# The first group of a streaming encoder's input projection: k by k over all three column tiles, with two weight pieces issued from ScalarE's queue

## The chip, the core and the metric

One core of a Trainium2 chip runs the whole program. The metric is the device time of one execution in microseconds (us). Five engines work side by side, each on its own row of instructions, in the order in which the program lists them: TensorE (PE, matmuls into PSUM), VectorE (DVE), ScalarE (ACT), GpSimd (POOL) and SyncE (SP), which issues nearly all DMAs of this kernel. They wait for one another through semaphores. PSUM is used as eight banks; the kernel gives six of them to the matmul results (pool `psm`) and two to small products.

## What is computed

One layer of a hybrid encoder over 2048 prompt positions and 8 x 16 sample positions, width 1024:

```python
h = jnp.einsum('btd,de->bte', x, w_in)                      # 1024 -> 2816 columns
a, g_a, u, v, g_b, c1, c2, g_c = jnp.split(h, SPLITS, axis=-1)
y_a = pool_mixer(pool_ext, a, ...)                           # trailing means, pool_w
y_b = u * spatial_mix(layer_norm(v), gmlp_w, gmlp_b)         # chunked gating
c = c1 * jax.nn.sigmoid(c2)
y_c = conformer_tail(concat(conv_left, c), conv_w, ...)      # 31 taps, LayerNorm, pointwise
mixed = concat([silu(g_a) * y_a, silu(g_b) * y_b, silu(g_c) * y_c])
x_new = layer_norm(ALPHA * x + einsum(mixed, w_out) + b_out)
```

## The kernel before

**Three products for one.** Each float32 operand is split into a high part (`xhi`, `whi`: a cast on ACT) and a low part (`xlo`, `wlo`: value minus high part, on DVE). `mm3` issues for every 128-row slice k of the contraction three matmuls per result: high times high (L208) and the two mixed ones (L209, L210). Its argument `outs` lists the results that are built together; the loop over k is outside, that over the results inside.

**Blocks and groups.** Positions go in three blocks of 768, 768 and 640; x is kept transposed in SBUF as `xhi`, `xlo` for one block. The columns of `w_in` go in eight groups (`GROUPS`); group 0 holds the column tiles c2/0, c1/0, c2/1, and group 1 holds c1/1, c2/2, c1/2. A block of 768 positions is two runs of 384 for each column tile, so one column tile of a block fills two PSUM banks.

**Evictions of c1 and c2.** `c_in` allocates the banks, issues the matmuls and then the evictions: for c2 a tanh on ACT (L474) from PSUM into `cext`; for c1 a product on DVE (L476, shown under the helper's line L131) that reads `cext` and PSUM. After c1, 31 taps of the depthwise convolution are put in a list, `fill`, from which the program hands one at a time to DVE. With one column tile in `todo`, `c_in` calls `mm3` once for each run of 384; with two, once for all their runs together.

**Weights.** A group's weights come in four pieces of two k each, through four stage buffers (tag `stage`, shared with the x rows at the start), and are split into a ring of six `whi`, `wlo` pairs. In the first block the split pieces are also stored to DRAM (`put`, L184, arrays `keep`), because the later blocks read them back. Group 0 and the x rows are loaded by code at the top (L280 to L303): `w0` is the first weight piece, loaded in two halves from inside `XRow` (its argument `mid`), between the two halves of the x rows 0 and 1. `Loader` loads the next group's pieces, and its `hook` splits the last two at given k of the last `mm3` of a group.

**What sets the order.** All engines are programmed by hand (`manual_schedule`). A planner's clock, `Clock.pe`, is moved on by `poll` after every k of `mm3`; `after(us, fn)` puts work on a list that `poll` takes from when its time has come. So what an engine's row holds, and in which order, follows from the places at which `poll` is called, and not from what is ready on the chip. The weights of the pooling mixer (`load_pool`, tile `pw`) are loaded 12 us into that plan by four DMAs on SP (L349) and split 8 us of the plan later (a cast on ACT, `poolwhi`, and a difference on DVE, `poolwlo`).

Of the kernel before, what the change touches and what calls it, by code (L numbers as in the profile page):

```python
# [11 lines left out]
AF = mybir.ActivationFunctionType  # L12
# [48 lines left out]
def splits(total):  # L61

    tiles = total // P
    n = -(-tiles // 3)
    out, t = [], 0
    for i in range(n):
        w = -(-(tiles - t) // (n - i))
        out.append((t * P, w * P))
        t += w
    return out  # L70
# [3 lines left out]
def encoder_kernel(ctx: ExitStack, tc: tile.TileContext, a):  # L74
    nc = tc.nc
# [28 lines left out]
    def drain(tag=None):  # L104

        while fill and (tag is None or any(t == tag for t, _ in fill)):
            fill.pop(0)[1]()

    def poll(us):
        Clock.pe += us  # L110
        while events and events[0][0] <= Clock.pe:
            heapq.heappop(events)[2]()
        run_fill()
# [22 lines left out]

    warm = const.tile([P, 1], F32, name="warm")
    nc.vector.memset(warm, 0.0)
    nc.scalar.activation(out=warm, in_=warm, func=AF.Silu)
    mhalf = const.tile([P, 1], F32, name="mhalf")  # L140
    nc.gpsimd.memset(mhalf, -0.5)
    onec = const.tile([P, 1], F32, name="onec")
# [20 lines left out]
    def stage():  # L163
        return core.tile([P, TMAX], F32, tag="stage", bufs=STAGE, name="stage")
# [33 lines left out]
    def wslice(key, k, c0, n):  # L198
        hi, lo = ring[key][k // 2]
        return hi[:, k % 2, c0:c0 + n], lo[:, k % 2, c0:c0 + n]  # L200

    def mm3(outs, kdim=KT, hook=None):

        for k in range(kdim):
            for ps, lhs, rhs in outs:
                lh, ll = lhs(k)
                rh, rl = rhs(k)
                nc.tensor.matmul(ps, lh, rh, start=(k == 0), stop=False)  # L208
                nc.tensor.matmul(ps, lh, rl, start=False, stop=False)  # L209
                nc.tensor.matmul(ps, ll, rh, start=False, stop=(k == kdim - 1))  # L210
            if hook is not None:
                hook(k)
            poll(sum(3 * (o[0].shape[-1] / 2400 + 0.0025) for o in outs))
        Clock.dve = max(Clock.dve, Clock.pe)
# [54 lines left out]
    def xslice(k, t0, n):  # L269
        return xhi[k // 2][:, k % 2, t0:t0 + n], xlo[k // 2][:, k % 2, t0:t0 + n]  # L270
# [10 lines left out]
    wv = a["w_in"][:, 0:KT * 384].rearrange("p (k c) -> p k c", k=KT)  # L281
    w0 = stage().rearrange("p (k c) -> p k c", k=2)
# [2 lines left out]
    ring[0, 0] = [(whi0, wlo0)]  # L285
    rows = []
    for k in range(2):
        rows.append(XRow(0, k, lambda k=k: nc.sync.dma_start(out=w0[:, k, :], in_=wv[:, k, :])))
    w1 = wg[1]()
    for k in range(2):  # L290
        nc.vector.tensor_copy(whi0[:, k, :], w0[:, k, :])
# [4 lines left out]
    for k in range(2, KT, 2):  # L296
        rows = [XRow(0, k), XRow(0, k + 1)]
# [142 lines left out]
    def prompt_width(b):  # L440
        return min(len(BLOCKS[b]), SEQ // P - BLOCKS[b][0]) * P

    def c_in(b, todo, wkey, hook=None):

        T, Tp = len(BLOCKS[b]) * P, prompt_width(b)
        runs, pss = [], {}
        for what, j, c0 in todo:
            if what == "c2":
                drain(j)
                ext = cp.tile([P, CONVC + TMAX], F32, tag=f"cext{j}", name=f"cext{j}")  # L450
                conv_state[(b, "ext", j)] = ext
                nc.gpsimd.tensor_copy(ext[:, 0:CONVC], halo_c[:, j, :])
            for t0, n in splits(T):
                ps = psm.tile([P, 512], F32, tag="mm", name="ps_c")
                pss[(what, j, t0)] = ps
                runs.append((ps[:, :n], lambda k, c0=c0: wslice(wkey, k, c0, P),
                             lambda k, t0=t0, n=n: xslice(k, t0, n)))
        if len(todo) > 1:
            mm3(runs)
        for what, j, c0 in todo:  # L460
            ext = conv_state[(b, "ext", j)]
            for t0, n in splits(T):
                if len(todo) == 1:
                    mm3([runs.pop(0)], hook=hook if t0 > 0 else None)
                ps = pss[(what, j, t0)]
                m = max(min(n, Tp - t0), 0)
                pieces = []
                if m > 0:
                    pieces.append((ext[:, CONVC + t0:CONVC + t0 + m], ps[:, :m]))
                if m < n:  # L470
                    pieces.append((exts[:, j, :, CONVC:], ps[:, m:n].rearrange("p (b t) -> p b t", b=NB)))
                for e, p in pieces:
                    if what == "c2":
                        nc.scalar.activation(out=e, in_=p, func=AF.Tanh, scale=0.5)  # L474
                    else:
                        vec.scalar_tensor_tensor(out=e, in0=e, scalar=1.0, in1=p,  # L476
                                                       op0=ALU.add, op1=ALU.mult)
            if what == "c1":
                nc.gpsimd.tensor_copy(halo_c[:, j, :], ext[:, Tp:Tp + CONVC])
                if conv_state.get("held") is None:  # L480
                    conv(b, j)
                else:
                    conv_state["held"].append(lambda j=j: conv(b, j))
# [167 lines left out]
    def spread(steps, every=STEP):  # L651

        def go():
            try:
                fn = next(steps)
            except StopIteration:
                return
            if fn is not None:
                fn()
            after(every, go)  # L660
        go()
# [179 lines left out]
    class Loader:  # L841
# [21 lines left out]
        def hook(self, plan):  # L863
            return lambda k: self.next(plan.get(k, 0))
# [3 lines left out]
    def group_work(b, g, hook):  # L868
        key, group = (b, g), GROUPS[g]
        what = group[0][0]  # L870
        if what in ("v", "gb", "u"):
            {"v": b_v, "gb": b_gate, "u": b_u}[what](b, key, hook)
        elif what in ("c1", "c2"):
            todo = [(w, j, c * P) for c, (w, j) in enumerate(group)]
            if g == 0:
                c_in(b, todo[:2], key)
                todo = todo[2:]
            for i, t in enumerate(todo):
                c_in(b, [t], key, hook if i == len(todo) - 1 else None)
        elif g == LASTG:  # L880
            c_gate(b, [(0, 0)], key)
            c_gate(b, [(1, P), (2, 2 * P)], key, hook)
        else:
            for c, (what, j) in enumerate(group):
                {"ga": a_gate, "a": a_main}[what](b, j, key, c * P, hook if c == len(group) - 1 else None)
# [3 lines left out]
    for b in range(len(BLOCKS)):  # L889
        if b > 0:  # L890
            drain()
            conv_state["held"] = []
            spread(tail_steps(b - 1))
        for g in range(LASTG):
            if b == 0 or (b, g + 1) == (LASTB, LASTG):
                loads = Loader([(fn, 1) for fn in w_in((b, g + 1), g + 1)])
                after(6, loads.next)
                after(9, loads.next)
                group_work(b, g, loads.hook({1: 1, 3: 1}))
            else:  # L900

                for i, fn in enumerate(w_kept(b, g + 1)):
                    after(10 + i if g % 2 == 0 and i < 2 else 5 + i, fn)
                group_work(b, g, None)
        if b == 0:
            W = w_kept(b + 1, 0)
            after(5, W[0])
            after(6, W[1])
            loads = Loader([(lambda k=k: XRow(b + 1, k), 1) for k in range(KT)])

            def leave(k):
                if k in (2, 4):
                    W[1 + k // 2]()
                if 2 <= k < 7:
                    loads.next()
            group_work(b, LASTG, leave)
            loads.next(3)
        elif b < LASTB:
            for i, fn in enumerate(w_kept(b + 1, 0)):
                after(5 + i, fn)  # L920
            rows = {}

            def load(*ks, b=b):
                for k in ks:
                    rows[k] = XRow(b + 1, k)

            def leave(k):
                if k in (2, 4):
                    load(k - 2, k - 1)
                if k == 5:  # L930
                    for i in range(2):
                        rows[i].split(lambda i=i: load(i + 4))
            group_work(b, LASTG, leave)
            for i in range(2, 4):
                rows[i].split(lambda i=i: load(i + 4))
            for i in range(4, KT):
                after((2.5, 3.5, 5.5, 6.5)[i - 4], lambda i=i: rows[i].split())
# [24 lines left out]
    wv = a["w_out"].rearrange("(k p) c -> p k c", p=P)  # L962
# [28 lines left out]
    loads = Loader(jobs)  # L991
# [176 lines left out]
```

## Time and profile before

| what | value |
|---|---|
| median of 3 runs | 785.02 us (785.01 to 785.61) |
| profiled execution, device time | 785.92 us |
| profiled execution, span | 784.2 us |
| PE busy, share of the span | 771.1 us, 98% |
| DVE busy, share of the span | 611.3 us, 78% |
| ACT busy, share of the span | 203.8 us, 26% |

The span runs from the first to the last instruction of the profiled execution; the device time beside it holds 1.72 us more. In a timeline row stand the start in us, the duration in us, the engine, the line, the operation with output and inputs, the count, and in brackets the idle time of the engine before it with what ended it. Matmuls overlap in time, so their pace is read from the differences of their starts. SPq is SP's queue: the time in which it issues a DMA, not that in which the data moves. PEld is the loading of the stationary operand.

### The profile page before, as it was taken

To read this page: it belongs to the slowest core of one execution; us is meant where nothing else is said; L and a number is where in the kernel's file an instruction comes from. 1 tells how busy PE (TensorE), PEld (TensorE's weight loads), DVE (VectorE), ACT (ScalarE), POOL (GpSimd) and SP (SyncE) were. 2 spreads that over 40 slices of the span, in tenths; PEclk is the share of its full clock that TensorE was granted. 3 is DMA by queue.
4 is the path that set the end of the run, shared out by engine and by line. 5 is a ranking of instruction groups with operands and counts; after the bars stand their busy time and mean duration, and the time that the engine had idled before them with its cause. 6 is when DMAs were issued, how large, how long until landed. Compare 5 with 4: busy or idle time off the path is not lost.

```text
span 784.2 us, 11348 instructions
## 1 busy us (share of the span) xinstructions
PE 771.1 (98%) x4340; PEld 732.4 (93%) x4340; DVE 611.3 (78%) x904; ACT 203.8 (26%) x380; POOL 146.3 (19%) x175
## 2 busy tenths in 40 slices
PE   8999999999999999999999999999999999999995
PEld 7999999999999999999999999999988878888885
DVE  5699999996489989896047888898764997676665
ACT  5322323222312130220142122031351243131210
POOL 1010112210011011230002200160006154232342
PEclk9999999999999999999999999999999999999999
DMA  7866856459431375413655147362477334435411
GB/s 259 329 217 189 279 218 231 160 192 344 172 109 53 81 237 187 161 55 132 230 172 199 58 103 209 134 209 97 143 230 266 108 134 162 161 116 176 137 71 61
DMA packets 74918, 132.91 MB, mean 169 GB/s; under 512 B 15600, under 2 KB 41712, under 8 KB 74864
## 3 DMA queue, kind: packets, MB, share of 16 engines
q1 hardware_dynamic: 74864, 132.19, 50.2%
q8 instruction: 34, 0.56, 0.3%
q14 instruction: 20, 0.16, 0.1%
HBM read 90.52 MB, written 41.64 MB: 169 GB/s over the span
## 4 chain that ended last, share of the span: by engine, by line
PE 87%; DVE 3%; DMA 3%; SPq 3%; ACT 1%; POOL 1%; issue 1%; POOLq 0%; DVEq 0%; ACTq 0%
PE ps_o L208 7%; PE ps_o L210 7%; PE ps_o L209 7%; PE ps_c L208 4%; PE ps_c L210 4%; PE ps_c L209 4%; PE ps_gb L208 3%; PE ps_gb L209 3%; PE ps_gb L210 3%; PE ps_v L209 3%; PE ps_v L210 3%; PE ps_v L208 3%; PE ps_u L210 3%; PE ps_u L209 3%; PE ps_u L208 3%; PE ps_gc L210 2%
## 5 line engine op out<-in xcount | busy, mean ns | idle before, releaser
L131 DVE SCALAR_TENSOR_TENSOR acc<-cext,cw,acc 128x768 f32<-128x768 f32 (+1 forms) x270 | 257.8, 955 | 4.2
L208 PE MATMUL ps_o<-woxhi,mhi 128*128 128x512 f32 (+1 forms) x208 | 81.5, 392 | 0.3 <-ACT sgc L533 0.3
L210 PE MATMUL ps_o<-woxhi,mlo 128*128 128x512 f32 (+1 forms) x208 | 80.7, 388 | 0.0
L208 PE MATMUL ps_c<-xhi,whi 128*128 128x384 f32 (+1 forms) x240 | 79.7, 332 | 0.4 <-ACT xhi L152 0.4
L209 PE MATMUL ps_o<-woxlo,mhi 128*128 128x512 f32 (+1 forms) x208 | 80.0, 385 | 0.0
L209 PE MATMUL ps_c<-xlo,whi 128*128 128x384 f32 (+1 forms) x240 | 79.1, 329 | 0.5 <-DVE xlo L131 0.5
L210 PE MATMUL ps_c<-xhi,wlo 128*128 128x384 f32 (+1 forms) x240 | 78.5, 327 | 0.0
L131 DVE TENSOR_TENSOR xlo<-stage,xhi 128x768 fp32r<-128x768 f32 (+2 forms) x26 | 21.6, 853 | 35.5 <-ACT xhi L152 35.5
L210 PEld LDWEIGHTS ps_o<-woxhi,mlo 128*128 128x128 f32 x208 | 39.0, 188 | 8.7
L209 PEld LDWEIGHTS ps_c<-xlo,whi 128*128 128x128 f32 x240 | 45.2, 188 | 1.8 <-DVE xlo L131 1.6
L208 PE MATMUL ps_u<-whi,xhi 128*128 128x384 f32 x136 | 46.6, 343 | 0.0
L208 PEld LDWEIGHTS ps_o<-woxhi,mhi 128*128 128x128 f32 x208 | 39.2, 188 | 7.9 <-ACT sgc L533 0.7
L209 PEld LDWEIGHTS ps_o<-woxlo,mhi 128*128 128x128 f32 x208 | 39.1, 188 | 8.0
L208 PEld LDWEIGHTS ps_c<-xhi,whi 128*128 128x128 f32 x240 | 45.4, 189 | 1.0 <-ACT xhi L152 0.7
L424 ACT ACTIVATE xr<-xr,onm,ors 128x1024 f32<-128x1024 f32 x16 | 19.9, 1246 | 99.9 <-POOL onm L420 99.9
L210 PE MATMUL ps_u<-whi,xlo 128*128 128x384 f32 x136 | 45.6, 335 | 0.0
L209 PE MATMUL ps_u<-wlo,xhi 128*128 128x384 f32 x136 | 45.5, 335 | 0.0
L209 PE MATMUL ps_v<-wlo,xhi 128*128 128x384 f32 x136 | 45.5, 334 | 0.0
L210 PE MATMUL ps_v<-whi,xlo 128*128 128x384 f32 x136 | 45.5, 334 | 0.0
L208 PE MATMUL ps_v<-whi,xhi 128*128 128x384 f32 x136 | 45.5, 334 | 0.0
L210 PEld LDWEIGHTS ps_c<-xhi,wlo 128*128 128x128 f32 x240 | 45.3, 189 | 0.0
L131 DVE TENSOR_TENSOR xr<-xr,ln_g 128x1024 f32<-128x1024 f32 x16 | 28.5, 1782 | 20.1 <-ACT xr L424 20.1
(216 smaller groups left out, 1947.2 us busy)
## 6 DMA issues: line engine op xcount, KB each, us to landing
whi<-keep SPq DMA_DIRECT2D x34, 384.0 KB, 5.5
wlo<-keep SPq DMA_DIRECT2D x34, 384.0 KB, 6.1
stage<-in_w_in SPq DMA_DIRECT2D x27, 384.0 KB, 5.0
keep<-whi SPq DMA_DIRECT2D x24, 384.0 KB, 3.9
keep<-wlo SPq DMA_DIRECT2D x24, 384.0 KB, 3.9
xr<-in_x_prompt SPq DMA_DIRECT2D x16, 512.0 KB, 4.8
o_y<-xr SPq DMA_DIRECT2D x16, 512.0 KB, 2.9
stage<-keep SPq DMA_DIRECT2D x20, 384.0 KB, 7.4
```

The lines of the kernel that those rows point to most:

```text
L131: return fn(*args, **kw)
L208: nc.tensor.matmul(ps, lh, rh, start=(k == 0), stop=False)
L209: nc.tensor.matmul(ps, lh, rl, start=False, stop=False)
L210: nc.tensor.matmul(ps, ll, rh, start=False, stop=(k == kdim - 1))
L424: nc.scalar.activation(out=out, in_=src, func=AF.Identity, scale=rs, bias=nm_)
```

## The change

Three edits. First, in block 0, group 0 is done by one call of `c_in` with all three column tiles: six runs, in six banks, k by k; before, the first two column tiles went k by k in four banks and the third followed by itself. `c_in` now hands its `hook` to that `mm3`. Second, the plan at which the next group's last two weight pieces are split becomes k = 5 and k = 7 of that one `mm3`; it was k = 1 and k = 3 of the last run. Third, the two halves of `w0` are issued from ACT's DMA queue and no longer from SP's, and the first activation on ACT (`warm`, a Silu of one column, which brings the loading of the activation table with it) is moved behind them.

```diff
-    nc.scalar.activation(out=warm, in_=warm, func=AF.Silu)
...
     for k in range(2):
-        rows.append(XRow(0, k, lambda k=k: nc.sync.dma_start(out=w0[:, k, :], in_=wv[:, k, :])))
+        rows.append(XRow(0, k, lambda k=k: nc.scalar.dma_start(out=w0[:, k, :], in_=wv[:, k, :])))
+    nc.scalar.activation(out=warm, in_=warm, func=AF.Silu)
...
         if len(todo) > 1:
-            mm3(runs)
+            mm3(runs, hook=hook)
...
-            if g == 0:
+            if g == 0 and b == 0:
+
+                c_in(b, todo, key, hook)
+                todo = []
+            elif g == 0:
                 c_in(b, todo[:2], key)
                 todo = todo[2:]
...
-                group_work(b, g, loads.hook({1: 1, 3: 1}))
+                group_work(b, g, loads.hook({1: 1, 3: 1} if (b, g) != (0, 0) else {5: 1, 7: 1}))
```

In the changed kernel the lines from L139 to L288 have numbers one smaller, so L207 to L209 there are the three matmuls, L151 the cast and L183 the stores of the kept weights.

On PE, at the end of the first k of group 0, the row of before reads as follows; the numbers behind `ps_c` name the banks' tiles.

```order
L208 MATMUL ps_c_235<-xhi0_110,whi_96 128x384
L209 MATMUL ps_c_235<-xlo0_111,whi_96 128x384
L210 MATMUL ps_c_235<-xhi0_110,wlo_97 128x384
L208 MATMUL ps_c_232<-xhi0_110,whi_96 128x384
L209 MATMUL ps_c_232<-xlo0_111,whi_96 128x384
L210 MATMUL ps_c_232<-xhi0_110,wlo_97 128x384
```

The same place of the changed kernel:

```order
L207 MATMUL ps_c_235<-xhi0_110,whi_95 128x384
L208 MATMUL ps_c_235<-xlo0_111,whi_95 128x384
L209 MATMUL ps_c_235<-xhi0_110,wlo_96 128x384
L207 MATMUL ps_c_238<-xhi0_110,whi_95 128x384
L208 MATMUL ps_c_238<-xlo0_111,whi_95 128x384
L209 MATMUL ps_c_238<-xhi0_110,wlo_96 128x384
L207 MATMUL ps_c_239<-xhi0_110,whi_95 128x384
L208 MATMUL ps_c_239<-xlo0_111,whi_95 128x384
L209 MATMUL ps_c_239<-xhi0_110,wlo_96 128x384
L207 MATMUL ps_c_232<-xhi0_110,whi_95 128x384
L208 MATMUL ps_c_232<-xlo0_111,whi_95 128x384
L209 MATMUL ps_c_232<-xhi0_110,wlo_96 128x384
```

Between the fourth bank and the return to the first one now stand the two banks of c2/1: a k holds 18 matmuls where it held 12, and all six banks are finished in the last k.

On ACT, around the end of group 0, the row of before with the semaphores that each instruction waits for (`cext_230` is column tile 0, `cext_364` column tile 1; `whi` of 128x768 are group 1's four pieces, `whi` of 128x2x256 the first of group 2's):

```order
L152 CAST whi<-stage 128x768 [waits DMAHW0_49]
L152 CAST whi<-stage 128x768 [waits DMAHW1_49]
L474 ACTIVATE cext_230<-ps_c 128x384 [waits PE_49] x2
L474 ACTIVATE cext_364<-ps_c 128x384 [waits PE_49]
L152 CAST whi<-stage 128x768 [waits DMAHW2_49,DMAHW4_49,DVE_49,PE_49]
L152 CAST whi<-stage 128x768 [waits DMAHW3_49,DMAHW6_49,DVE_49,PE_49]
L152 CAST poolwhi<-pw_338 128x256 [waits DMAHW6_49,DMAHW1_49,DMAHW7_49,DMAHW0_49,Pool_49]
L474 ACTIVATE cext_364<-ps_c 128x384 [waits PE_49]
L152 CAST whi<-stage 128x2x256 [waits DMAHW6_49,DMAHW2_49]
```

The same place now (`cext_236` is column tile 1):

```order
L151 CAST whi<-stage 128x768 [waits DMAHW0_49]
L151 CAST whi<-stage 128x768 [waits DMAHW1_49]
L151 CAST whi<-stage 128x768 [waits DMAHW2_49,DMAHW4_49,DVE_49,PE_49]
L151 CAST whi<-stage 128x768 [waits DMAHW3_49,DMAHW6_49,DVE_49,PE_49]
L151 CAST poolwhi<-pw_347 128x256 [waits DMAHW6_49,DMAHW1_49,DMAHW7_49,DMAHW0_49,Pool_49]
L474 ACTIVATE cext_230<-ps_c 128x384 [waits PE_49] x2
L474 ACTIVATE cext_236<-ps_c 128x384 [waits PE_49] x2
L151 CAST whi<-stage 128x2x256 [waits DMAHW6_49,DVE_49]
```

Three of the four tanh evictions have moved behind group 1's last two weight casts and behind the cast of the pool weights, which waits for the four DMAs of `pw`.

On SP, at the very start, the row of before:

```order
L257 DMA stage<-in_xT 128x384
L288 DMA stage<-in_w_in 128x384
L259 DMA stage<-in_xT 128x384
L257 DMA stage<-in_xT 128x384
L288 DMA stage<-in_w_in 128x384
L259 DMA stage<-in_xT 128x384
L172 DMA stage<-in_w_in 128x768
```

And now:

```order
L256 DMA stage<-in_xT 128x384
L258 DMA stage<-in_xT 128x384
L256 DMA stage<-in_xT 128x384
L258 DMA stage<-in_xT 128x384
L171 DMA stage<-in_w_in 128x768
```

The two weight halves are gone from SP's row. Behind this place SP's row is the same in both kernels: the rest of x and of group 0, `cst`, group 1's four pieces, ten stores of kept weights, the four DMAs of `pw`, and so on. On DVE all four differences of group 1's pieces now stand ahead of the two products of c1/0, and the first taps follow these.

## The prediction

> **What bounds the kernel now.** I read the page first: busy shares, then the chain of work that ended last.
>
> ```profile
> PE 771.1 (98%) x4340; PEld 732.4 (93%) x4340; DVE 611.3 (78%) x904; ACT 203.8 (26%) x380; POOL 146.3 (19%) x175
> PE 87%; DVE 3%; DMA 3%; SPq 3%; ACT 1%; POOL 1%; issue 1%; POOLq 0%; DVEq 0%; ACTq 0%
> ```
>
> PE is the bound: the end of the kernel moves by what PE's row of work moves, and anything else counts only through a wait of PE. So the next view is the timeline of PE over the first 62 us, where the change lies.
>
> ```profile
> 4.48 0.88 PE L208 MATMUL ps_c<-xhi,whi 128*128 128x384 f32 x1
> ...
> 6.01 0.34 PE L208 MATMUL ps_c<-xhi,whi 128*128 128x384 f32 x1
> ...
> 9.84 0.34 PE L210 MATMUL ps_c<-xhi,wlo 128*128 128x384 f32 x1
> 10.56 0.45 PE L208 MATMUL ps_c<-xhi,whi 128*128 128x384 f32 x1 [0.38 <-ACT xhi L152]
> 11.55 0.44 PE L209 MATMUL ps_c<-xlo,whi 128*128 128x384 f32 x1 [0.55 <-DVE xlo L131]
> 11.83 0.34 PE L210 MATMUL ps_c<-xhi,wlo 128*128 128x384 f32 x1
> ...
> 32.34 0.33 PE L208 MATMUL ps_c<-xhi,whi 128*128 128x384 f32 x1
> ...
> 57.30 0.33 PE L208 MATMUL ps_ga<-xhi,whi 128*128 128x384 f32 x1
> ...
> 59.56 0.34 PE L209 MATMUL ps_ga<-xlo,whi 128*128 128x384 f32 x1
> 60.33 0.44 PE L210 MATMUL ps_ga<-xhi,wlo 128*128 128x384 f32 x1 [0.43 <-DVE wlo L131]
> ```
>
> Group 1 runs from 32.34 to 57.30 without a wait: 144 matmuls in 24.96 us, 0.1733 us each. Group 0 has the same 144 and took 32.34 - 4.48 = 27.86 us, so it loses **2.90 us**. Of these, 1.01 lie in the first three matmuls (the fourth starts at 6.01, not at 5.00), 1.48 at 9.84 to 11.83 (three steps in 1.99 us where 0.52 would do), where x row 2 arrives late, and 0.4 in between. A last loss is at 60.33, 0.60 us behind its pace (0.77 after 59.56 less 0.17), on a low weight part that DVE made late. More than 3 us can't be won here.
>
> **The change, part by part.** *k by k over six banks.* A k holds 18 matmuls, 3.12 us, where it held 12, 2.08 us. Rows on DVE that end x rows 2, 4 and 7:
>
> ```profile
> 10.54 0.96 DVE L131 TENSOR_TENSOR xlo<-stage,xhi 128x768 fp32r<-128x768 f32 x1 [0.83 <-ACT xhi L152]
> ...
> 14.38 0.96 DVE L131 TENSOR_TENSOR xlo<-stage,xhi 128x768 fp32r<-128x768 f32 x1
> 20.64 0.96 DVE L131 TENSOR_TENSOR xlo<-stage,xhi 128x768 fp32r<-128x768 f32 x1 [0.78 <-ACT xhi L152]
> ```
>
> With 1.0 us lost at the start as now, k = 2 begins at 4.48 + 1.0 + 36 x 0.1733 = 11.7 and its x row is there at 11.50; k = 4 at 18.0 against 15.34, k = 7 at 27.3 against 21.60. All are met even if no row comes earlier. Group 0 then ends at 4.48 + 24.96 + 1.0 = **30.4**, a gain of 1.9.
>
> *Two issues on ACT's queue.*
>
> ```profile
> 0.78 1.28 ACT L139 ACT_TABLE_LOAD   x1 [0.78 <-PEq L1150]
> 2.08 0.20 ACT L139 ACTIVATE warm<-warm 128x1 f32<-128x1 f32 x1
> 3.21 0.51 ACT L152 CAST xhi<-stage 128x384 fp32r<-128x384 f32 x1 [0.93 <-DMA stage<-in_xT]
> ...
> 1.24 0.42 SPq L288 DMA_DIRECT2D stage<-in_w_in  x1
> ...
> 2.64 0.43 SPq L288 DMA_DIRECT2D stage<-in_w_in  x1
> ```
>
> The table load and `warm` move behind two issues of 0.42 and 0.43, to end near 3.2; ACT was idle 0.93 us there waiting for the first x half, so that cast stays near 3.2 and costs nothing, and would cost PE nothing until it slips by about 0.5. SP gives up 0.85 us, so everything behind may come 0 to 0.85 us earlier; the lower end, if the engines that move the data are full, the upper if only issuing counts. I take 0.5, since the stage buffers and the data both hold the row.
>
> *The evictions of group 0.* This is the large term. ACT's row now:
>
> ```profile
> 22.76 0.84 ACT L152 CAST whi<-stage 128x768 fp32r<-128x768 f32 x1 [0.95 <-DMA stage<-in_w_in]
> 23.50 0.87 ACT L474 ACTIVATE cext<-ps_c 128x384 f32<-128x384 f32 x2
> ...
> 30.29 0.84 ACT L152 CAST whi<-stage 128x768 fp32r<-128x768 f32 x1 [1.41 <-PE ps_c L209]
> 31.33 0.84 ACT L152 CAST whi<-stage 128x768 fp32r<-128x768 f32 x1 [0.20 <-PE ps_c L209]
> 37.12 0.41 ACT L152 CAST poolwhi<-pw 128x256 fp32r<-128x256 f32 x1 [4.95 <-DMA pw<-in_pool_w]
> 37.44 0.49 ACT L474 ACTIVATE cext<-ps_c 128x384 f32<-128x384 f32 x1
> ```
>
> ACT waits 4.95 us for the pool weights, and today that is harmless: the tanhs that free group 1's first banks ran at 23.50, ahead of it, and only one stands behind it. In the changed order the pool cast stands ahead of all four. Group 0 holds six banks of six, all unfinished until the last k, so group 1's first matmul needs the first tanh, and that needs the pool weights. When do they land?
>
> ```profile
> 22.00 1.52 SPq L184 DMA_DIRECT2D keep<-whi  x1
> ...
> 31.13 0.77 SPq L184 DMA_DIRECT2D keep<-wlo  x1
> 31.99 3.31 SPq L349 DMA_DIRECT2D pw<-in_pool_w  x4
> ...
> 24.00:32.30 8.30, 8.30 (x50) 8.30 (x49) 7.33 (x10) 2.54 (x4) 0.72 (x2) 1.00 0.99 397
> ```
>
> On SP they stand behind ten stores of kept weights (the first and the last shown), in a stretch whose DMA engines are 0.99 busy at 397 GB/s; SP's order there is unchanged, and none of those stores waits for PE. So they come when they come now, less the 0.5. The weight casts ahead of the pool cast wait for stores too, but these are ahead of `pw` on SP, and the casts had run by 32.2.
> - pool cast: 37.12 - 0.5 = 36.6; first tanh 37.44 - 0.5 = 36.94, end 37.43;
> - group 1 starts at about **37.45**: PE stands still for 37.45 - 30.4 = 7.0 us, and group 1 begins 37.45 - 32.34 = **5.1 us later** than before.
>
> Behind the waiting pool cast stand on ACT the four tanhs, then group 2's casts; on DVE the two products of c1/0, `poolwlo` and the first taps; on POOL the halo copies. Group 2's weights aren't needed until 62.
>
> *Restart of PE.* A pause of 7 us has no like in the trace. The lower bound is the pause at 9.84 to 11.83, after which the pace was full at once: 0. The upper is the start of the program:
>
> ```profile
> 3.56 0.15 PEld L277 LDWEIGHTS <-wz 128*128 128x128 bf16 x1 [0.28 <-issue]
> 3.99 0.15 PEld L277 LDWEIGHTS <-wz 128*128 128x128 bf16 x1 [0.28 <-issue]
> ...
> 1.45 3.60 PE L277 MATMUL wps<-wz 128*128 128x512 bf16 x8 [1.45 <-POOL wz L274]
> ...
> 3.75:5.00 1.25, 1.25 (x5) 0.49 (x2) 1.19 (x3) 0.02 (x1) 0.00 (x0) 1.00 0.81 230
> ```
>
> There the warm-up matmuls of 512 columns follow one another every 0.43 us, 0.32 for 384 columns where 0.173 is the later pace, and this holds from 1.45 to about 6.0: 4.55 x (1 - 0.173 / 0.32) = 2.1 us lost. Seven idle microseconds are nearer to that than to two; I take **1.9**. The granted clock speaks against it: the third number from the end of the window row is 1.00 there too, so that column doesn't show what slowed PE.
>
> The Trainium skill has a rule for it ("TensorE: Matmul & The Clock Gate", section "What's actually happening"): PE's clock falls to half after an idle window of about 3.4 us and returns after one of sustained work. By it the slow stretch would be an estimated 3.4 to 6.8 us and the loss 1.6 to 3.1; the head's pace agrees with it, the granted clock column doesn't.
>
> *The taps.* DVE starts the convolution at about 38.5 instead of 25.6. By then it had done six taps:
>
> ```profile
> 25.63 0.68 DVE L131 TENSOR_SCALAR acc<-cext,cw,cst 128x768 f32<-128x768 f32 x1
> 26.34 4.18 DVE L131 SCALAR_TENSOR_TENSOR acc<-cext,cw,acc 128x768 f32<-128x768 f32 x4
> ...
> 33.08 1.01 DVE L131 SCALAR_TENSOR_TENSOR acc<-cext,cw,acc 128x768 f32<-128x768 f32 x1
> ...
> 59.59 1.29 DVE L131 TENSOR_TENSOR wlo<-stage,whi 128x512 fp32r<-128x512 f32 x2
> ...
> 80.00:100.00 20.00, 20.00 (x118) 20.00 (x117) 19.58 (x25) 6.25 (x10) 1.99 (x3) 1.00 0.85 287
> 180.00:200.00 20.00, 20.00 (x117) 20.00 (x116) 11.08 (x13) 7.13 (x12) 0.00 (x0) 1.00 0.95 334
> ```
>
> That is 0.68 + 4.18 + 1.01 = 5.9 us put off, while PE itself is 7 us later, and in the new order seven taps fewer (17, not 24) stand ahead of the `wlo` of 59.59. So the stall of 0.60 at 60.33 should go, and the taps end in the 8.9 us that DVE idles in 180 to 200. I cost it at -0.6; without that cover it is 0.
>
> **Sum**, against the profiled execution: 785.92 + 5.1 + 1.9 - 0.6 = 792.3. That execution is 0.90 above the median of the runs, so on the median: 785.02 + 6.4 = **791.4 us**. Nothing after 62 us would win it back, PE being without slack.
>
> **The rivals.**
> - *No slow restart.* All as above, but PE resumes at full pace: 791.4 - 1.9 = **789.5**. For it: the pause at 10 us. Against it: that pause is short. Chance 0.22.
> - *DVE's backlog bites.* From 80 us DVE is nearly full, and the taps put off may stand ahead of a weight difference or of an eviction that PE waits for. The price is between the 0.6 not won back and the 5.9 put off; I take 2: **793.4**. Against it: the plan moved the taps behind those. Chance 0.12.
> - *The wait isn't there, and it is faster.* If the pool weights land early enough, PE goes on and the change brings 1.9 + 0.6: **782.5**. The point from which it decides: group 1 starting by 32.34 + 0.6, five microseconds before 37.95, that is the weights in SBUF by about 32.1. Before, SP only began to issue them at 31.99, and 0.85 is the most that the change brings forward. It needs the full DMA engines to be emptied by much more than two issues. Chance 0.07.
> - *Something between*: landing 2 to 4 us earlier, a shorter pause, no slow restart: about **786.5**. Chance 0.04.
>
> **How the numbers follow.** The forecast itself has 0.55. A measurement of this kernel tells about 0.2%, 1.6 us, from no change: faster 0.07, same 0.03, slower 0.90. The range: low end, no slow restart and the full 0.85 won, 789.5 - 0.35, less 0.35 for a start that loses 0.65 instead of 1.0: 788.8. High end: no shift (+0.5), restart 2.1 (+0.2), the stall of 60.33 kept (+0.6), and half of the first microsecond of the backlog case: 793.2. What is left out are the last two rivals and the larger part of the second.
>
> **What would show it.** Right: group 0's last matmul near 30.4 with no wait at 10 to 12; the pool cast near 36.6 with a wait for `pw` ahead of it; on PE one idle gap of about 7 us that ends on a tanh of ACT; matmuls of 384 columns every 0.32 us for some microseconds behind it; no wait on `wlo` near 66. Wrong: a pool cast before 32, a gap under 5 us, full pace at once, or PE waits for DVE after 62 us that weren't there.

## The result and the profile after

| kernel | median, us | lowest to highest | runs |
|---|---|---|---|
| before | 785.02 | 784.45 to 785.73 | 5 |
| changed | 791.75 | 790.72 to 792.17 | 5 |

The changed kernel is slower: ratio 1.0082, 95% interval 1.0070 to 1.0093. (This and the later ratios are formed over all the runs and differ a little from the quotient of two medians.) The profiled execution took 792.17 us (span 790.5), 6.25 more than the one of before (785.92, span 784.2). The page's busy shares and the shares of the chain that ended last:

```profile
PE 771.6 (98%) x4340; PEld 734.1 (93%) x4340; DVE 611.8 (77%) x904; ACT 203.2 (26%) x380; POOL 145.4 (18%) x175
PE 84%; DMA 5%; DVE 4%; POOL 2%; SPq 1%; ACT 1%; issue 1%; POOLq 0%; ACTq 0%; DVEq 0%
```

The busy times are those of before to within a microsecond (PEld: 1.7), so the 6.25 us are no added work. PE is still the bound, and DMA's share of the chain has grown from 3% to 5%. The timeline of PE says where:

```profile
4.51 0.46 PE L207 MATMUL ps_c<-xhi,whi 128*128 128x384 f32 x1
5.48 0.44 PE L208 MATMUL ps_c<-xlo,whi 128*128 128x384 f32 x1 [0.51 <-DVE xlo L131]
5.94 0.33 PE L207 MATMUL ps_c<-xhi,whi 128*128 128x384 f32 x1
...
30.23 0.34 PE L209 MATMUL ps_c<-xhi,wlo 128*128 128x384 f32 x1
37.44 0.69 PE L207 MATMUL ps_c<-xhi,whi 128*128 128x384 f32 x1 [6.87 <-ACT cext L474]
37.92 0.52 PE L208 MATMUL ps_c<-xlo,whi 128*128 128x384 f32 x1
...
41.44 0.52 PE L207 MATMUL ps_c<-xhi,whi 128*128 128x384 f32 x1
41.76 0.43 PE L208 MATMUL ps_c<-xlo,whi 128*128 128x384 f32 x1
42.03 0.34 PE L209 MATMUL ps_c<-xhi,wlo 128*128 128x384 f32 x1
42.21 0.34 PE L207 MATMUL ps_c<-xhi,whi 128*128 128x384 f32 x1
...
64.57 0.33 PE L207 MATMUL ps_ga<-xhi,whi 128*128 128x384 f32 x1
```

Group 0 ends at 30.40 (its last start, 30.23, and one step of 0.17), without the waits of 10 to 12 us. Group 1 begins at 37.44: 7.04 us of standstill, ended by a tanh of ACT. (The 6.87 in the bracket is counted from the end of the last matmul, which overlaps the next step.) Then the starts are 0.48, twelve times 0.32 and once 0.27 us apart before they are 0.17 to 0.18. Group 1 takes 64.57 - 37.44 = 27.13 us, 2.17 more than the 24.96 of before. What held the tanh stands in ACT's timeline, one row above it:

```profile
3.83 0.51 ACT L151 CAST xhi<-stage 128x384 fp32r<-128x384 f32 x1 [0.63 <-DMA stage<-in_xT]
...
29.18 0.83 ACT L151 CAST whi<-stage 128x768 fp32r<-128x768 f32 x1 [1.06 <-DMA keep<-whi]
36.59 0.41 ACT L151 CAST poolwhi<-pw 128x256 fp32r<-128x256 f32 x1 [6.57 <-DMA pw<-in_pool_w]
36.90 1.63 ACT L474 ACTIVATE cext<-ps_c 128x384 f32<-128x384 f32 x4
```

All four tanhs are queued behind the cast of the pool weights. The chain of waits between 28 and 45 us joins the pieces; a row is the start, the length and what it was:

```profile
30.07 1.04 SPq L349
...
32.05 0.59 SPq L349
32.64 0.04 issue
32.68 3.76 DMA pw<-in_pool_w
...
36.59 0.41 ACT poolwhi L151
36.99 0.40 ACT cext L474
37.39 0.04 issue
37.44 0.69 PE ps_c L207
```

SP issues the four DMAs of `pw` (L349) from 30.07 on, the last of them needs 3.76 us to land, and the cast, the first tanh and PE follow it with no more than 0.15 us between them.

The windows show the state of PE behind the standstill and the room on DVE. Columns: stretch, length, busy time of PE, PEld, DVE, ACT and POOL with counts, granted clock, DMA share, GB/s.

```profile
30.00:37.00 7.00, 0.57 (x4) 0.24 (x2) 0.96 (x1) 0.43 (x3) 0.00 (x0) 0.87 0.93 365
38.25:39.50 1.25, 1.25 (x5) 1.25 (x5) 1.21 (x4) 0.28 (x1) 0.26 (x1) 0.50 0.99 312
80.00:100.00 20.00, 20.00 (x117) 20.00 (x117) 17.95 (x25) 7.51 (x14) 1.73 (x3) 1.00 0.84 279
180.00:200.00 20.00, 20.00 (x119) 19.96 (x118) 18.47 (x20) 4.67 (x8) 0.00 (x0) 1.00 0.89 314
```

Behind the standstill the granted clock is 0.50. In windows of 0.5 to 1.5 us it is still 1.00 up to 35, has a mean of 0.57 from 35 to 36, is 0.50 from 36 to 41.5 and 1.00 again from 42: it fell about 4.7 us after group 0's end and came back about 4.5 us after PE had resumed. DVE, with 11.08 us of work in 180 to 200 before, now has 18.47 there, and 17.95 instead of 19.58 in 80 to 100.

PE's waits in the first 700 us, grouped: who waits for whom, the sum, the count, the longest.

```profile
PE ps_c L207 <- ACT cext L474: 6.9, 1, 6.9
PE wps L276 <- POOL wz L273: 1.4, 1, 1.4
PE ps_rstd L600 <- ACT crs L594: 1.1, 1, 1.1
PE tp_b L748 <- ACT yt L750: 0.8, 1, 0.8
PE ps_c L208 <- DVE xlo L131: 0.5, 1, 0.5
```

Rows two, three and four were there before, to about a tenth. No wait for `wlo` is left, and none for DVE after 62 us.

### The profile page after: what moved, and what is told of

Same layout as the page of the kernel before. It is cut to its first block, busy times and chain, and to the rows that moved or that the text cites. A ratio compares the mean times of both kernels' runs of the same rounds, so it can differ in the third digit from the quotient of the medians.

```text
span 790.5 us, 11348 instructions
## 1 busy us (share of the span) xinstructions
PE 771.6 (98%) x4340; PEld 734.1 (93%) x4340; DVE 611.8 (77%) x904; ACT 203.2 (26%) x380; POOL 145.4 (18%) x175
## 4 chain that ended last, share of the span: by engine, by line
PE 84%; DMA 5%; DVE 4%; POOL 2%; SPq 1%; ACT 1%; issue 1%; POOLq 0%; ACTq 0%; DVEq 0%
PE ps_o L207 6%; PE ps_o L209 5%; PE ps_o L208 5%; PE ps_c L207 5%; PE ps_c L209 5%; PE ps_c L208 5%; PE ps_gb L207 3%; PE ps_gb L208 3%; PE ps_gb L209 3%; PE ps_v L208 3%; PE ps_v L209 3%; PE ps_v L207 3%; PE ps_u L208 3%; PE ps_u L209 3%; PE ps_u L207 3%; PE ps_gc L208 2%
## 5 line engine op out<-in xcount | busy, mean ns | idle before, releaser
L207 PE MATMUL ps_c<-xhi,whi 128*128 128x384 f32 (+1 forms) x240 | 80.3, 334 | 6.9 <-ACT cext L474 6.9
L207 PE MATMUL ps_o<-woxhi,mhi 128*128 128x512 f32 (+1 forms) x208 | 81.4, 392 | 0.1
L209 PE MATMUL ps_o<-woxhi,mlo 128*128 128x512 f32 (+1 forms) x208 | 80.7, 388 | 0.0
L209 PE MATMUL ps_c<-xhi,wlo 128*128 128x384 f32 (+1 forms) x240 | 79.2, 330 | 0.0
L207 PEld LDWEIGHTS ps_c<-xhi,whi 128*128 128x128 f32 x240 | 45.8, 191 | 7.5 <-ACT cext L474 7.2
L209 PEld LDWEIGHTS ps_o<-woxhi,mlo 128*128 128x128 f32 x208 | 39.0, 188 | 8.7
L207 PE MATMUL ps_u<-whi,xhi 128*128 128x384 f32 x136 | 46.6, 343 | 0.0
L207 PEld LDWEIGHTS ps_o<-woxhi,mhi 128*128 128x128 f32 x208 | 39.2, 188 | 7.7 <-ACT sgc L533 0.5
L209 PEld LDWEIGHTS ps_c<-xhi,wlo 128*128 128x128 f32 x240 | 45.8, 191 | 0.0
L209 PE MATMUL ps_u<-whi,xlo 128*128 128x384 f32 x136 | 45.6, 335 | 0.0
L209 PE MATMUL ps_v<-whi,xlo 128*128 128x384 f32 x136 | 45.5, 334 | 0.0
L207 PE MATMUL ps_v<-whi,xhi 128*128 128x384 f32 x136 | 45.5, 334 | 0.0
```

## Experiments

The theory: the slowdown is ACT's order. The pool cast stands ahead of the four tanhs; it holds them until the pool weights land; PE then restarts slowly. The six banks by themselves are a gain. The rivals: the order of six banks costs in itself (a burst of evictions, taps put off on DVE); issuing from ACT's queue costs; the moved pool weights would be worth the same without the six banks. For each ratio below, the kernel before was run again on the same chip as the experiment; its medians there are 785.30 to 785.41 us.

### The pool cast behind the tanhs

The cast is handed out 9.2 us of the plan after the load and not 8, which puts it behind group 0's evictions on ACT. Against the changed kernel:

```diff
-        after(8, lambda: split(*pw, w))
+        after(9.2, lambda: split(*pw, w))
```

> Changed kernel with the pool weights' cast due 9.2 us instead of 8 us after their load in the plan, so that it stands directly behind the four tanhs on ACT, not ahead of them. Theory (group 1 waits for a bank whose tanh queues behind the pool cast): PE's gap of 7.04 us shrinks to about 0.5 (the last weight cast ends near 30.0, then one tanh), no slow restart; 791.75 - 6.6 - 2.2 = 783.0, up to 783.6 if DVE, which still waits for the pool weights, makes a weight difference late near 58. Rival (holding all six banks to the last k is what costs, whatever stands on ACT): the gap stays over 5 us and the time over 789.

Measured: 783.41 us (783.02 to 783.83) against 785.41 of before, ratio 0.9972 [0.9962, 0.9983]. ACT's timeline:

```profile
28.51 0.84 ACT L151 CAST whi<-stage 128x768 fp32r<-128x768 f32 x1 [1.06 <-DMA keep<-whi]
29.25 0.87 ACT L474 ACTIVATE cext<-ps_c 128x384 f32<-128x384 f32 x2
30.29 1.01 ACT L474 ACTIVATE cext<-ps_c 128x384 f32<-128x384 f32 x2 [0.17 <-PE ps_c L209]
35.97 0.41 ACT L151 CAST poolwhi<-pw 128x256 fp32r<-128x256 f32 x1 [4.67 <-DMA pw<-in_pool_w]
```

and PE's:

```profile
30.44 0.33 PE L209 MATMUL ps_c<-xhi,wlo 128*128 128x384 f32 x1
30.61 0.33 PE L207 MATMUL ps_c<-xhi,whi 128*128 128x384 f32 x1
...
55.57 0.33 PE L207 MATMUL ps_ga<-xhi,whi 128*128 128x384 f32 x1
```

The wait for the pool weights is still on ACT, 4.67 us long, but nothing that PE needs stands behind it: group 1 begins at 30.61, one step after group 0, and takes 24.96 us. There is no gap at all, where 0.5 was expected: the first column tile's two banks are finished early in the last k, and their tanhs (29.25 to 30.12) run while PE still works on the other four. Against the changed kernel `ps_ga` begins 64.57 - 55.57 = 9.00 us earlier: 6.83 because group 1 begins earlier and 2.17 of slow pace. One cast in another place thus takes the whole loss away, and with six banks the kernel is faster than before.

### The pool weights loaded earlier

The cast keeps its place ahead of the tanhs, but `pw` is issued ahead of the ten stores on SP. (The second number counts from the load, so the cast falls due at about the same time of the plan.)

```diff
-        after(8, lambda: split(*pw, w))
+        after(19, lambda: split(*pw, w))
...
-    after(12, load_pool)
+    after(2, load_pool)
```

> Changed kernel with the pool weights loaded ahead of the ten stores on SP, the pool cast at its old place ahead of the tanhs. Theory (the landing sets the gap, the place on ACT alone does not): pool cast right behind the last weight cast near 30, one tanh, group 1 starts near 31.3, no slow restart: 783.5. Rival (the cast's place or the eviction of six banks costs by itself): over 789.

Measured: 783.15 us (782.36 to 783.89), ratio 0.9969 [0.9958, 0.9981]. ACT's timeline:

```profile
28.54 0.83 ACT L151 CAST whi<-stage 128x768 fp32r<-128x768 f32 x1 [1.18 <-DMA keep<-whi]
29.28 0.40 ACT L151 CAST poolwhi<-pw 128x256 fp32r<-128x256 f32 x1
29.59 1.63 ACT L474 ACTIVATE cext<-ps_c 128x384 f32<-128x384 f32 x4
```

and PE's, where group 0 goes over into group 1:

```profile
30.34 0.33 PE L209 MATMUL ps_c<-xhi,wlo 128*128 128x384 f32 x1
30.52 0.33 PE L207 MATMUL ps_c<-xhi,whi 128*128 128x384 f32 x1
```

Group 1 begins at 30.52, one step after group 0 (31.3 was expected). On ACT the cast of the pool weights still stands ahead of the four tanhs, as in the changed kernel, and the loss is gone: not the order alone is the cause, but the order with the late landing. The two runs take away one condition each, and each is enough.

### PE kept busy through the gap

Thirty matmuls whose result nobody reads stand between group 0 and group 1; all else is as changed.

```diff
+                wp2 = pst.tile([P, 512], F32, tag="tr", name="wp2")
+                for _ in range(30):
+                    nc.tensor.matmul(wp2, wz[:, 0:P], wz, start=True, stop=True)
```

> Changed kernel with 30 dummy matmuls of 512 columns on PE behind group 0 (about 6.5 us of the 7.0 us gap), everything else in its place. Theory (PE runs at half pace behind the gap because it was idle): group 1 still starts near 37.4 but takes 24.96 us instead of 27.1: 791.75 - 2.2 = 789.6. Rival (the slow stretch comes from what runs beside it, DMA traffic or ACT's evictions): group 1 stays at 27 us, 791.7.

Measured: 790.2 us (789.14 to 791.35), ratio 1.0059 [1.0046, 1.0073]. PE's timeline:

```profile
31.11 6.65 PE L881 MATMUL wp<-wz 128*128 128x512 bf16 x30
38.87 0.44 PE L207 MATMUL ps_c<-xhi,whi 128*128 128x384 f32 x1 [1.11 <-ACT cext L474]
39.15 0.33 PE L208 MATMUL ps_c<-xlo,whi 128*128 128x384 f32 x1
...
63.96 0.33 PE L207 MATMUL ps_ga<-xhi,whi 128*128 128x384 f32 x1
```

Group 1 takes 63.96 - 38.87 = 25.09 us instead of 27.13, and the window from 38.87 to 40.25 has a granted clock of 1.00 where the changed kernel's had 0.50. So the slow pace comes from PE's having stood still; the 1.11 us for which it still stood here brought no such stretch. In this profile the pool cast ran at 38.02, 1.43 later than in the changed kernel's, which hides most of the gain in its span (789.6). The ratios differ by 1.0082 - 1.0059, some 1.8 us; their intervals just overlap.

### The two issues back on SP

The changed kernel without its third edit (`w0` on SP's queue, `warm` at the top):

```diff
+    nc.scalar.activation(out=warm, in_=warm, func=AF.Silu)
...
-        rows.append(XRow(0, k, lambda k=k: nc.scalar.dma_start(out=w0[:, k, :], in_=wv[:, k, :])))
-    nc.scalar.activation(out=warm, in_=warm, func=AF.Silu)
+        rows.append(XRow(0, k, lambda k=k: nc.sync.dma_start(out=w0[:, k, :], in_=wv[:, k, :])))
```

> Changed kernel with the two weight halves back on SP's queue and the first activation back at the top. Theory (the second queue brings all that follows on SP about 0.5 us forward, the pool weights too): the pool cast near 37.1, 792.2. Rival (two queues at once make the first x half land later, 3.8 instead of 3.2, and that eats the gain): 791.3 to 791.8.

Measured: 792.5 us (790.52 to 793.17), ratio 1.0083 [1.0070, 1.0096]. ACT's timeline:

```profile
3.15 0.51 ACT L152 CAST xhi<-stage 128x384 fp32r<-128x384 f32 x1 [0.88 <-DMA stage<-in_xT]
...
37.20 0.40 ACT L152 CAST poolwhi<-pw 128x256 fp32r<-128x256 f32 x1 [6.58 <-DMA pw<-in_pool_w]
```

The pool cast is 0.61 later than in the changed kernel's profile, in the direction of the theory, but the times can't be told apart (1.0083 and 1.0082). PE restarts slowly here too: group 1 takes from 38.04 to 64.83, 26.79 us, so 1.83 are lost. The issue on ACT is no cause of the loss; inside the changed kernel its own effect isn't resolved.

### Each edit alone, on the kernel before

First the issue from ACT's queue alone: the third edit's three lines of the diff of the change, nothing else.

> Kernel of before with only the two weight halves on ACT's queue and the first activation behind them. Theory (the second queue brings x rows and weights about 0.5 us forward, and PE waits for them at 10 to 12): that wait shrinks from 1.5 us to about 1.0, ratio 0.9994. Rival (the first x half comes 0.6 us later and eats it): ratio 1.000.

Measured: 784.33 us (783.88 to 785.26), ratio 0.9989 [0.9980, 0.9997]: a small gain. But PE's waits at x row 2 are nearly as before, where the theory had them shrink from 1.5 to about 1.0 us:

```profile
10.21 0.45 PE L207 MATMUL ps_c<-xhi,whi 128*128 128x384 f32 x1 [0.30 <-ACT xhi L151]
11.21 0.44 PE L208 MATMUL ps_c<-xlo,whi 128*128 128x384 f32 x1 [0.55 <-DVE xlo L131]
```

Both rows stand 0.34 to 0.35 earlier, and `ps_ga` begins at 56.90, 0.40 earlier than before. The wait for `wlo` at 60.33 is absent from this profile as well. Which of these makes the gain isn't shown.

Then the six banks alone: the first two edits, `w0` on SP's queue, and the pool cast behind the tanhs (the diffs of the fourth and of the first run, together).

> Changed kernel with the pool cast behind the tanhs and the two weight halves back on SP's queue: k by k over six banks alone. Theory (two separate gains: the six banks take away the waits for x row 2, the second queue brings the start forward): the six banks alone give about two thirds of what both give, ratio 0.998. Rival (the second queue adds nothing once the six banks have taken the waits away): ratio 0.997, as with both.

Measured: 783.65 us (782.90 to 786.71), ratio 0.9982 [0.9972, 0.9991]. PE has no wait in its first 60 us but that of the warm-up. The rival's 0.997 lies just outside the interval. The two parts multiply to 0.9982 x 0.9989 = 0.9971, and the first run with both had 0.9972. They add, though the intervals are wide beside the queue's part.

### The pool weights moved, with and without six banks

The cast, and the load of the next weights behind it, later still in the changed kernel:

```diff
-        after(8, lambda: split(*pw, w))
+        after(18, lambda: split(*pw, w))
...
-    after(24, load_v)
+    after(34, load_v)
```

> Changed kernel with the pool weights' split due 18 us after their load and the next user of their buffer, load_v, 10 us later in the plan, so that neither ACT nor DVE waits for them. Theory (group 0's gain of 1.9 and the stall of 0.6 at 60 are all there is): PE runs from 5.5 to past 80 without a wait, 785.0 - 2.5 = 782.5, ratio 0.9968. Rival (DVE's earlier start of the taps wins more, or the moved loads collide later): below 0.9955, or over 0.998.

Measured: 783.34 us (782.79 to 783.41), ratio 0.9973 [0.9962, 0.9984], the same as with 9.2; the 0.9968 of the theory lies inside the interval. With 9.2 DVE stood for 4.26 us at `poolwlo`, here it doesn't: that wait of DVE costs nothing that can be measured.

The same two lines in the kernel before, and then the early load (the second run's two lines) in the kernel before:

> Kernel of before with the same two plan times moved (18 us, and load_v 10 us later), four banks and the third column tile by itself as before. Theory (before loses 0.6 us at 60.33 because DVE had waited for the pool weights): that stall goes, group 0's loss of 2.9 stays: ratio 0.9992. Rival (the moved pool weights are what makes the kernels of the experiments fast, not the six banks): ratio under 0.998.

> Kernel of before with the pool weights loaded ahead of the ten stores. Same question as with the late split: theory, only the stall of 0.6 at 60.33 goes, ratio 0.9992; rival, the early load is what made the changed kernel fast with it, ratio under 0.998.

Measured: 785.23 and 785.07 us, ratios 0.9999 [0.9990, 1.0008] and 0.9996 [0.9987, 1.0004], no gain in either, though 0.9992 lies inside both intervals. The wait at 60.33 is gone in both profiles: from `ps_ga` to `ps_gb` they take 60.35 us, where before took 61.08. But `ps_ga` itself begins 0.75 and 0.70 later than in the profile of before. In the second one x row 2 came later, and the wait for it was longer:

```profile
11.29 0.44 PE L208 MATMUL ps_c<-xhi,whi 128*128 128x384 f32 x1 [0.90 <-ACT xhi L152]
```

That is long before SP reaches the moved load (21.88), so it is the scatter of single profiles. So moving the pool weights by itself is worth nothing that can be measured here; the 0.27 to 0.31% of the three runs of the changed kernel with the pool weights moved need the six banks.

## Why the prediction was right

The time (791.4 forecast, 791.75 measured) came out of the steps as given. On the profiled executions: 5.10 (later begin of group 1) + 2.17 (slow restart) - 0.73 (between `ps_ga` and `ps_gb`) - 0.29 (later) = 6.25 us.

- *Group 0 ends at 30.4.* Right: 30.40, no wait at 10 to 12. That it agrees to the hundredth is luck: in the seven profiles with six banks group 0 ends at 30.40 to 31.32, in the four with four banks at 31.94 to 33.09. The means are 1.7 apart, near the gain of 1.9. (Of the loss at 9.84 to 11.83, 1.99 - 0.52 is 1.47 and not 1.48.)
- *The pool cast holds the evictions.* Right in place and size (cast 36.6 forecast, 36.59 measured; gap 7.0 and 7.04), and shown from both sides by the first two runs. What the wait costs over the same kernel without it is 8.3 us by the medians (791.75 and 783.41), 8.6 by the two ratios.
- *The shift of 0.5.* It measured 0.53, and that it came so near is luck. Over the runs the pool cast, where it waits for its weights behind the ten stores, lies between 35.66 and 38.02, in seven profiles, so a shift of 0.5 is inside the scatter of single profiles and isn't settled. SP itself reached `pw` 1.92 us earlier (30.07 against 31.99), more than the upper bound of 0.85; but this too is partly scatter. Where `pw` stands behind the ten stores, SP begins the first of them at 21.98 to 22.56 in the four profiles with `w0` on SP's queue and at 20.92 to 21.49 in the five with it on ACT's (1.06 apart in the mean), and from there to `pw` it takes between 9.00 and 10.03 us, whichever queue it is. That the full DMA engines hold the landing is argued from the window (0.93 busy), and wasn't tried by itself.
- *Slow restart 1.9.* Right in kind; 2.17 in size. The first interval of 0.48 alone loses 0.31, the twelve of 0.32 lose 1.76, the last 0.10. The fourth run's profile lost 1.83, so the two lie on either side of the 1.9 taken. In both the granted clock is low for an estimated 6.8 us (worked out from the means of windows of 1 us; 35.1 to 42.0 and 35.0 to 41.8); in the fourth run PE resumed later within that stretch (38.04 against 37.44) and lost less. The Trainium skill's rule ("TensorE: Matmul & The Clock Gate", section "What's actually happening") agrees: half pace for some 4.5 us (37.44 to 41.9) and 3.8 us in the fourth run, both inside the estimate given, and none where the gap was filled.
- *"The granted clock speaks against it."* This argument was empty: that column is 1.00 at the head, where PE is slow, and 0.50 after the gap. It shows the slow pace in one place and not in the other; why, no run shows.
- *The stall at 60.33 goes, -0.6.* Right for the two profiles: -0.73 over the stretch to `ps_gb` (7.27 later at 64.57, 6.54 later at 124.92). But of the four profiles with four banks only that of before itself has this stall (61.08 us from `ps_ga` to `ps_gb`, 60.35 in the other three), and the two runs that moved the pool weights with four banks gained nothing that can be measured. So on the medians the -0.6 isn't shown.
- *Nothing after 62 us is won back.* Right as far as can be told: from `ps_gb` to the end of the span the changed kernel takes 665.58 us, before 665.82, and the eleven profiles lie between 664.78 and 665.82. So the last 0.29 is inside the scatter. The wait of 0.3 for `sgc` (a gate, from an activation on ACT) near 578 us in before is gone in the changed kernel, but it is back (0.5) in the first run, and so not the change's doing.
- *The first x cast stays near 3.2.* Wrong: 3.83. It cost nothing, since PE's fourth matmul starts at 5.94, against 6.01 before.
- *The taps end in DVE's idle time.* Right: in the window of 180 to 200 DVE has fifteen taps where it had six.
- *The rivals.* "No slow restart" and "DVE's backlog" fell in the trace. "The wait isn't there" did not occur, but its price was near: a gain of 2.5 forecast, 2.0 to 2.3 us between the medians in the first two runs. "Something between" did not occur.

The version to keep is the change with the pool cast behind the tanhs, or with the early load: about 2 us faster than before, 8.3 to 8.6 faster than the change. The two, and the late cast, can't be told apart.

## What to carry to other kernels

When a loop is widened until it holds all the banks, look at what stands on the evicting engine between the last matmul and the first eviction: a harmless wait there can become a standstill of PE, and a long one (here 7 us, not 1.1) is charged a second time in the slow restart. Before giving such a change up, move the waiting instruction behind the evictions, or its load forward; here one number in the plan turned 0.8% slower into 0.3% faster.

## What was not expected of the hardware

- The granted clock reads 1.00 in the first microseconds, in which matmuls of 512 columns follow one another every 0.43 us, and 0.50 behind a standstill of 7.04 us, with matmuls of 384 columns every 0.32 us: the same pace for each column, with two readings.
- With two queues in use at the start the first x half lands later, though SP issues it at the same 0.79 us; ACT is idle ahead of its cast, waiting for it (0.63 us in the changed kernel's profile). The first x cast lies at 3.72 to 4.08 us in the six profiles with the issue on ACT's queue, and at 3.04 to 3.31 in the five with SP's alone. Why isn't shown.
- SP's time for issuing isn't constant. A store of kept weights takes from 0.42 to 1.88 us to issue in the first run's profile (DMA share 0.99 from 21 to 31 us), and four DMAs of 16 KB take 3.0 to 3.4 us together in the nine profiles in which they stand behind the ten stores. So where SP arrives ten DMAs later depends on more than the number of issues. The Trainium skill ("DMA: Bandwidth & Descriptors", section "Issuing engines are not separate DMA queues") has it that issuing from several engines saves only the issuer's time. SP's first store came 1.06 us earlier in the mean for 0.85 handed over, which agrees in size.
